# Two-layer decoder kernel: the order of work on all five engines and the buffer slots come from a list scheduler in the kernel

## The chip, the cores and the metric

The kernel runs on one core of one Trainium2 chip. The metric is the device time of one execution in microseconds (us); the number compared is the median over several executions. Engines are named as in the profile: PE is the matrix engine (TensorE), with PEld for its weight loads; DVE is VectorE, ACT is ScalarE, POOL is GpSimd, and SP is the engine that issues nearly all DMA transfers.

## The reference

The kernel computes a two-layer decoder trunk for one sequence of 256 positions and width 1024, in float32. Each layer mixes tokens, then runs a SwiGLU block, each with a residual scaled by alpha and a LayerNorm:

```python
for i in range(DEPTH):                       # DEPTH = 2
    if i % N_MIXERS == 0:                    # layer 0: gated MLP over positions
        h = x @ a_w_in[li]
        u, v, q_mem = jnp.split(h, [W_MIX, 2 * W_MIX], axis=-1)
        mix = gmlp_mixer(u, v, a_ln_v_g[li], a_ln_v_b[li], a_w_s[li], a_b_s[li])
    else:                                    # layer 1: causal attention, 12 heads of 64
        h = x @ b_w_in[li]
        q, k, v, q_mem = jnp.split(h, [W_MIX, 2 * W_MIX, 3 * W_MIX], axis=-1)
        mix = moba_attention(q, k, v)        # 256 positions: one block, so plain causal
    mem_out = memory_cross_attention(q_mem, mem, w_mem_kv[i])   # 4 heads, 256 memory tokens
    sub = jnp.concatenate([mix, mem_out], axis=-1) @ w_mix_out[i]
    x = layer_norm(ALPHA * x + sub, ln_mix_g[i], ln_mix_b[i])
    x = layer_norm(ALPHA * x + swiglu(x, w_ffn_in[i], w_ffn_out[i]), ln_ffn_g[i], ln_ffn_b[i])
```

`gmlp_mixer` is gelu(u) * (W_s layer_norm(gelu(v)) + b_s), with a causal 128 x 128 matrix W_s for each of 12 groups; `swiglu` is (silu(g) * u) @ w_out with an inner width of 2816.

## The kernel before, in words

**Split weights.** PE works on float32 data in three passes. Every operand is split into a high part, which ACT makes by a cast to a shorter float type (line 248, `scalar.copy`), and a low part, which DVE makes by subtracting the high part from the original (line 249, `vector.tensor_sub`). A product is then high x high, high x low and low x high, all added up in PSUM. So every weight tile passes DMA, then ACT, then DVE, before PE can use both parts. Nearly all of the 117 MB that are read are weights; most come in tiles of 128 x 2048 floats (1 MB), each split in two halves of 128 x 1024.

**Tiles by name.** A tile `raw_x` is what a DMA loaded, and `spl_x_0`, `spl_x_1` are its two split halves. In the order of use: `raw_v0` to `raw_v3` (projection v of layer 0), `qm0` (memory queries), `u0` to `u2` (projection u), `km0` and `vm0` (memory keys and values; the memory tokens come as `mraw0` to `mraw3`), `o0_0` to `o0_3` (output projection), then the feed-forward weights of layer 0. Layer 1 has `bv0` to `bv3`, `qk0` to `qk5` (queries and keys, one tile for each pair of heads) and `o1_0` to `o1_3`. `wsT` and `vn<-in_bs` are the spatial matrices and broadcast biases of the gated MLP, and `gv` its norm's gain and shift.

**Keys with their low part.** Attention scores use stacked tiles: ACT casts the keys out of PSUM twice (lines 478 and 479, tiles `kkm` and `qks`), and DVE subtracts to get the low part, `klm` for the memory keys and `klq` for attention (line 480). The score product (tile `sm` or `s`) reads them at once.

**Feed-forward chunks.** The inner width is worked off in 11 chunks of 256. Chunks marked R are plain products; those marked S (four in each layer) use seven products M1 to M7 of sums of weight blocks (`raw_s1_7_11`, `_12`, `_21`, `_22` for layer 1, chunk 7). The sums are made in place by DVE (line 199, 128 x 2048) and by one accumulating DMA from POOL (line 202). Results of the products are joined by DVE at lines 625 to 636: tiles `m1g`, `u2g`, `m5g` for the gate half, and `m1f`, `m5f` for the other.

**What sets the order.** PE's order is that of the program text (`manual_schedule` for PE alone). The other engines' order is chosen by the framework's own scheduler, from the dependencies and from rotating pools: 4 raw tiles, 10 split tiles, 9 work tiles, and 4 + 4 PSUM tiles. At the output projection of layer 1, `stream.behind` with `issue_after` holds some splits behind named exponentials (line 206). Each engine works through its queue strictly in order, so an instruction that waits holds all that stand behind it on that engine. All loads named here are issued on SP's queue, save the accumulating ones.

## Time and profile before

| what | value |
| --- | --- |
| median of 3 runs | 563.2 us (562.88, 563.20, 563.69) |
| span of the profiled execution, first to last instruction | 561.0 us |
| around the span, against the median | 2.2 us (the profile gives no time of its own for that execution) |
| PE busy | 550.9 us, 98% of the span |
| PE weight loads busy | 478.4 us, 85% |
| DVE busy | 500.5 us, 89% |
| ACT busy | 360.1 us, 64% |
| POOL busy | 22.4 us, 4% |
| DMA | 118.88 MB, mean 212 GB/s |
| granted PE clock | 0.998 of full speed, mean over the core's span |

A row of the waits view reads: the engine that waited, the tile it was to produce and its line, the engine and tile waited for, then the time in total, how many times, and the longest. A row of the timeline reads: start and duration in us, engine, line, operation, output<-inputs, shapes and count (several instructions of one kind in a row are one row), and in brackets the idle time before it with what ended it. A row of the windows view gives for a stretch of time the busy time and instructions of each engine, the granted clock, the mean busy share of the 16 DMA engines, and what they moved in GB/s.

### The profile page before, as it was taken

What the parts mean: (1) busy time and instruction counts of PE and PEld (TensorE: products, weight loads), DVE (VectorE), ACT (ScalarE), POOL (GpSimd) and SP (SyncE); (2) the same over time, 40 slices, a digit from 0 to 9 for tenths busy, and PEclk for the clock granted to TensorE, in tenths of its full rate; (3) what the DMA queues carried; (4) which work ended last, traced back from release to release, by engine and by line L of the source; (5) the groups of instructions that cost most, each with busy time, mean ns of one, the idle gap of its engine ahead of it and who ended that gap; (6) DMA issues with size and microseconds to landing.
All of it is one profiled execution on the core that took longest, in us unless ns stands there. A gap on an engine that the chain in (4) does not pass through costs nothing.

```text
span 561.0 us, 8037 instructions
## 1 busy us (share of the span) xinstructions
PE 550.9 (98%) x3052; PEld 478.4 (85%) x3052; DVE 500.5 (89%) x667; ACT 360.1 (64%) x550; POOL 22.4 (4%) x32
## 2 busy tenths in 40 slices
PE   8999999999999999999999999999999999999994
PEld 8999979888888888888899999788888887888883
DVE  5897999999998999995987879789998997999985
ACT  6766947767655766863466879765676674765910
POOL 2020000000000000000000000000000000000001
PEclk9999999999999999999999999999999999999999
DMA  8997794548756486598477222367258766485602
GB/s 291 399 324 308 250 369 170 208 77 313 210 206 247 112 325 161 192 335 296 140 240 297 75 77 76 142 254 280 85 152 316 197 249 217 133 307 145 225 1 75
DMA packets 21623, 118.88 MB, mean 212 GB/s; under 512 B 2384, under 2 KB 6096, under 8 KB 9168
## 3 DMA queue, kind: packets, MB, share of 16 engines
q1 hardware_dynamic: 20000, 109.45, 52.8%
q0 software_dynamic: 1152, 8.39, 8.1%
q8 instruction: 24, 0.39, 0.3%
q10 hardware_dynamic: 432, 0.52, 0.3%
q14 instruction: 15, 0.12, 0.1%
HBM read 117.31 MB, written 1.05 MB: 211 GB/s over the span
## 4 chain that ended last, share of the span: by engine, by line
PE 85%; DVE 7%; ACT 3%; DMA 2%; issue 2%; SPq 1%; DVEq 0%; ACTq 0%
PE fof L272 11%; PE fog L272 8%; PE Xf L272 8%; PE pg L272 6%; PE pf L272 6%; PE Xg L272 5%; PE opc L272 4%; PE opa L272 4%; PE Zf L272 4%; PE qk L272 4%; PE pu L272 3%; PE bv L272 3%; PE Zg L272 3%; PE pvm L272 3%; PE va L272 2%; PE hkm L272 2%
## 5 line engine op out<-in xcount | busy, mean ns | idle before, releaser
L248 ACT CAST spl_s_M<-raw_s 128x1024 fp32r<-128x1024 f32 x112 | 114.4, 1052 | 56.7 <-DVE raw_s L199 41.9
L249 DVE TENSOR_TENSOR spl_s_M<-raw_s,spl_s_M 128x1024 fp32r<-128x1024 f32 x112 | 132.6, 1217 | 7.7 <-ACT spl_s_M L248 7.5
L272 PE MATMUL fof<-spl_w,htf 128*128 128x512 f32 x264 | 63.8, 392 | 0.0
L272 PE MATMUL fog<-spl_w,htg 128*128 128x512 f32 (+1 forms) x282 | 63.7, 378 | 0.0
L272 PEld LDWEIGHTS fog<-spl_w,htg 128*128 128x128 f32 x282 | 50.2, 188 | 9.4
L272 PEld LDWEIGHTS fof<-spl_w,htf 128*128 128x128 f32 x264 | 49.0, 188 | 10.0
L199 DVE TENSOR_TENSOR raw_s<-raw_s,raw_s 128x2048 f32<-128x2048 f32 x24 | 54.8, 2284 | 0.2
L249 DVE TENSOR_TENSOR spl_w<-raw_w,spl_w 128x1024 fp32r<-128x1024 f32 x44 | 53.0, 1217 | 1.2 <-ACT spl_w L248 1.1
L248 ACT CAST spl_w<-raw_w 128x1024 fp32r<-128x1024 f32 x44 | 45.4, 1050 | 4.7 <-PE fog L272 1.9
L272 PE MATMUL qk<-x2T,spl_qk 128*128 128x256 f32 x288 | 36.3, 283 | 0.0
L272 PEld LDWEIGHTS qk<-x2T,spl_qk 128*128 128x128 f32 x288 | 35.2, 192 | 0.0
L272 PE MATMUL Xf<-spl_s_M,SfM 128*128 128x512 f32 x96 | 23.1, 389 | 0.0
L272 PE MATMUL opc<-spl_o,mix 128*128 128x512 f32 x96 | 23.1, 394 | 0.0
L272 PE MATMUL Zf<-spl_s_M,SfM 128*128 128x512 f32 x96 | 23.1, 389 | 0.0
L272 PE MATMUL Zg<-spl_s_M,SgM 128*128 128x512 f32 x96 | 23.1, 389 | 0.0
L272 PE MATMUL Xg<-spl_s_M,SgM 128*128 128x512 f32 x96 | 23.1, 389 | 0.0
L272 PE MATMUL Xg<-spl_s_M,x3T 128*128 128x512 f32 x96 | 22.7, 391 | 0.2 <-DVE m5g L632 0.2
L272 PE MATMUL Xf<-spl_s_M,x1T 128*128 128x512 f32 x96 | 22.6, 389 | 0.0
L272 PE MATMUL opa<-spl_o,mix 128*128 128x512 f32 x96 | 22.5, 392 | 0.0
L272 PEld LDWEIGHTS Xg<-spl_s_M,x3T 128*128 128x128 f32 x96 | 17.9, 188 | 4.4 <-DVE m5g L632 0.6
L272 PEld LDWEIGHTS Xf<-spl_s_M,SfM 128*128 128x128 f32 x96 | 18.0, 188 | 3.8
L272 PEld LDWEIGHTS Xg<-spl_s_M,SgM 128*128 128x128 f32 x96 | 18.0, 188 | 3.7
(245 smaller groups left out, 1080.2 us busy)
## 6 DMA issues: line engine op xcount, KB each, us to landing
raw_s<-in_w SPq DMA_DIRECT2D x32, 1024.0 KB, 5.1
raw_w<-in_w SPq DMA_DIRECT2D x22, 1024.0 KB, 4.8
raw_o<-in_w SPq DMA_DIRECT2D x8, 1024.0 KB, 6.3
raw_s<-in_w POOLq DMA_DIRECT2D x8, 1024.0 KB, 7.9
raw_r_A<-in_w SPq DMA_DIRECT2D x6, 1024.0 KB, 4.9
raw_r_B<-in_w SPq DMA_DIRECT2D x6, 1024.0 KB, 6.0
raw_qk<-in_w SPq DMA_DIRECT2D x6, 1024.0 KB, 5.5
raw_u<-in_w SPq DMA_DIRECT2D x3, 1024.0 KB, 9.2
```

Source lines behind the costliest of these rows:

```text
L199: self.nc.vector.tensor_add(self.raw[parts[0]], self.raw[parts[0]], self.raw[parts[1]])
L248: nc.scalar.copy(hi, src)
L249: nc.vector.tensor_sub(lo, src, hi.bitcast(F32))
L272: nc.tensor.matmul(o, lhsT, rhs, start=start, stop=stop, skip_group_check=on)
```

## The change

All of `build` is now recorded before it is issued. `nc` becomes a `Plan`: each call makes an `Op` with its engine, its operands, the operations that must precede it (found by overlap of the bytes of its operands) and a cost from a formula. `tile_of` makes a `Buffer` with a tag and a number of slots. At the end `nc.emit()` finds an order and issues it.

- `deadlines` goes along PE's order, which stays the program's, and gives each PE operation a time; then it goes backwards and gives every other operation the latest time by which it must start.
- `simulate` runs the machine by the cost formulas. At each step an engine takes, among operations that can start, the one with the earliest deadline; it may put in a shorter one, or wait a little, for a more urgent one that is about to be ready. Five sets of three limits are tried, and the order in which PE loses least is kept.
- A transfer is modelled as 2300 ns and a shared link at 437 bytes per ns.
- `emit` issues the operations in that order on all five engines (`manual_schedule` names all five), with a pool slot of its own for each tag and slot number, chosen by the same model.
- `stream.behind` and its `issue_after` are gone, since the order is explicit.

The methods `either`, `copy` and `scale`, which would let the scheduler choose between two engines, are not called; every operation stays on its engine, and PE's sequence is that of before.

```diff
 class Plan:
+    TRIALS = ((150, 1500, 800), (150, 1000, 500), (300, 1500, 1200), (100, 700, 300), (300, 2500, 1600))
...
+    def delay(self, a, b):
+        if a.engine == b.engine and a.name != "dma_start":
+            return a.hold
+        if a.name == "dma_start":
+            return 2300 + a.bytes / 400 if a.engine != "gpsimd" else 2300 + a.bytes / 180
+        return a.lat + (50 if b.engine == "tensor" else 33)
+
+    def deadlines(self):
+        t = 4300
+        for op in self.ops:
+            if op.engine == "tensor":
+                op.late = t
+                t += op.hold
...
+        for op in reversed(self.ops):
+            late = [o.late - self.delay(op, o) for o in op.after if o.late is not None]
+            late += [follow[b].late - self.delay(op, follow[b]) for b in op.roots if b in follow]
...
+            op.late = min(late) if late else t
...
+    def simulate(self, slip, idle, margin):
...
+                t0 = min(t for t, _ in c)
+                first = [x for x in c if x[0] <= t0 + 1]
+                t, op = min(first, key=lambda x: (x[1].late, x[1].n))
...
+            if op.name == "dma_start":
+                size = op.bytes * (2.1 if e == "gpsimd" else 1) / 437
+                link = max(link, t + 2300) + size
+                end = max(link, t + 7800 if e == "gpsimd" else 0) + 100
+            else:
+                end = t + op.call.lat
...
+    def emit(self):
...
+        for op in self.order():
+            for b in op.opens:
+                b.tile = self.pools[b.pool].tile(b.dims, b.dtype, tag=f"{b.tag}_{b.slot}", name=b.name, bufs=1)
+            c = op.call
+            getattr(getattr(self.nc, c.engine), c.name)(*map(real, c.args), **{k: real(v) for k, v in c.kw.items()})
...
-        if key in self.behind:
-            with self.tc.issue_after(self.behind[key]):
-                self.split(hl[:, 0, :n], hl[:, 1, :n], raw)
-        else:
-            self.split(hl[:, 0, :n], hl[:, 1, :n], raw)
+        self.split(hl[:, 0, :n], hl[:, 1, :n], raw)
...
-        tc.manual_schedule(engines={ET.PE}),
+        tc.manual_schedule(engines={ET.PE, ET.DVE, ET.Activation, ET.Pool, ET.SP}),
...
-        stream.behind = {(f"o1_{k}", x): prs[p][1].exp.ins for k, p in ((0, 2), (1, 3), (3, 4)) for x in range(2)}
```

Three places of the new order follow. In the rows the first item is the source line; after the change all recorded operations are issued by one helper, so they all have line 527. The number at the end of a tile's name is that of the buffer.

**SP, the first loads after those of projection v.** Before:

```order
L185 DMA raw_qm0_294<-in_w 128x2048
L185 DMA raw_u0_296<-in_w 128x2048
L185 DMA raw_u1_298<-in_w 128x2048
L185 DMA raw_u2_300<-in_w 128x2048
L185 DMA raw_km0_308<-in_w 128x2048
L768 DMA gv_310<-in_a_ln_v_g 128x768
L773 DMA mraw0_313<-in_memT 128x2x256
L781 DMA wsT_322<-in_wsT 128x1536
L789 DMA wsT_322<-in_bs 64x256 x4
L789 DMA vn_321<-in_bs 64x256 x2
L185 DMA raw_vm0_419<-in_w 128x2048
```

SP in the same place after the change:

```order
L527 DMA raw_qm0_192<-in_w 128x2048
L527 DMA mraw0_197<-in_memT 128x2x256
L527 DMA wsT_221<-in_wsT 128x1536
L527 DMA raw_u0_228<-in_w 128x2048
L527 DMA wsT_221<-in_bs 64x256 x4
L527 DMA vn_253<-in_bs 64x256
L527 DMA raw_u1_260<-in_w 128x2048
L527 DMA raw_u2_279<-in_w 128x2048
L527 DMA gv_285<-in_a_ln_v_g 128x768
L527 DMA raw_km0_321<-in_w 128x2048
L527 DMA raw_vm0_394<-in_w 128x2048
```

Rows that only repeat are left out: the second `gv`, `mraw1` to `mraw3`, and in the new order the second `vn<-in_bs`, between `raw_u1` and `raw_u2`. The same transfers stand between `raw_qm0` and `raw_vm0`, but `mraw`, `wsT` and the broadcasts have moved ahead of `raw_u0` to `raw_u2`, and `raw_km0` is the last of them instead of the fourth.

**DVE ahead of the memory scores.** Before, from the splits of `vm0` to the fourth `klm`:

```order
L249 TENSOR_TENSOR spl_vm0_0_730<-raw_vm0_419,spl_vm0_0_730 128x1024
L249 TENSOR_TENSOR spl_vm0_1_745<-raw_vm0_419,spl_vm0_1_745 128x1024
L249 TENSOR_TENSOR spl_o0_0_0_849<-raw_o0_0_478,spl_o0_0_0_849 128x1024
L249 TENSOR_TENSOR spl_o0_0_1_858<-raw_o0_0_478,spl_o0_0_1_858 128x1024
L480 TENSOR_TENSOR klm_126<-hkm0_591,kkm00_589 64x256
L828 TENSOR_TENSOR gt0_689<-sv0_680,wsT_322 128x512
L828 TENSOR_TENSOR gt1_705<-sv1_696,wsT_322 128x512
L480 TENSOR_TENSOR klm_126<-hkm0_591,kkm00_589 64x256
```

DVE after the change, from the splits of `km0` on; `vn` is the norm of the gated MLP:

```order
L527 TENSOR_TENSOR spl_km0_0_473<-raw_km0_321,spl_km0_0_473 128x1024
L527 TENSOR_TENSOR spl_km0_1_485<-raw_km0_321,spl_km0_1_485 128x1024
L527 BN_AGGR mvv0_514<-stv0_354 128x2
L527 SCALAR_TENSOR_TENSOR vn_253<-vn_253,mvv0_514,gv_285 128x768
L527 TENSOR_TENSOR spl_vm0_0_504<-raw_vm0_394,spl_vm0_0_504 128x1024
L527 TENSOR_TENSOR spl_o0_0_0_542<-raw_o0_0_437,spl_o0_0_0_542 128x1024
L527 TENSOR_TENSOR spl_o0_1_0_570<-raw_o0_1_468,spl_o0_1_0_570 128x1024
L527 TENSOR_TENSOR spl_o0_2_0_620<-raw_o0_2_521,spl_o0_2_0_620 128x1024
L527 TENSOR_TENSOR spl_o0_3_0_685<-raw_o0_3_600,spl_o0_3_0_685 128x1024
L527 TENSOR_TENSOR klm_116<-hkm0_635,kkm00_701 64x256
L527 TENSOR_TENSOR gt0_719<-sv0_698,wsT_221 128x512
L527 TENSOR_TENSOR klm_116<-hkm0_635,kkm01_722 64x256 x2
```

Left out are the second halves of `vm0`, `o0_0`, `o0_1` and `o0_2`, the second pair of statistics, three more `vn` steps, and the second `klm`, right behind `gt0`. Seven halves of `o0` now stand ahead of the first `klm` (two before), together with the `km0` splits and four `vn` steps, which before were over earlier; the second `gt` products and the `mix` splits that stood between the `klm` are behind them now.

**DVE at feed-forward chunk 7 of layer 1.** Before:

```order
L629 TENSOR_TENSOR u2g5_4444<-u2g5_4444,Zg5_4298 128x512
L630 SCALAR_TENSOR_TENSOR m1g5_4317<-m1g5_4317,u2g5_4444 128x512
L249 TENSOR_TENSOR spl_s1_7_M1_0_4534<-raw_s1_7_11_4510,spl_s1_7_M1_0_4534 128x1024
L249 TENSOR_TENSOR spl_s1_7_M1_1_4543<-raw_s1_7_11_4510,spl_s1_7_M1_1_4543 128x1024
L249 TENSOR_TENSOR spl_w1_4_1_4568<-raw_w1_4_4336,spl_w1_4_1_4568 128x1024
L199 TENSOR_TENSOR raw_s1_7_11_4510<-raw_s1_7_11_4510,raw_s1_7_12_4512 128x2048
L632 TENSOR_TENSOR m5g5_4370<-m5g5_4370,Xg5_4296 128x512
```

After the change:

```order
L527 TENSOR_TENSOR spl_s1_7_M1_0_4458<-raw_s1_7_11_4423,spl_s1_7_M1_0_4458 128x1024
L527 TENSOR_TENSOR spl_s1_7_M1_1_4464<-raw_s1_7_11_4423,spl_s1_7_M1_1_4464 128x1024
L527 TENSOR_TENSOR m1g5_4343<-m1g5_4343,Yg5_4416 128x512
L527 TENSOR_TENSOR u2g5_4481<-u2g5_4481,Zg5_4375 128x512
L527 TENSOR_TENSOR raw_s1_7_11_4423<-raw_s1_7_11_4423,raw_s1_7_12_4381 128x2048
L527 SCALAR_TENSOR_TENSOR m1g5_4343<-m1g5_4343,u2g5_4481 128x512
L527 TENSOR_TENSOR spl_w1_4_1_4473<-raw_w1_4_4280,spl_w1_4_1_4473 128x1024
L527 TENSOR_TENSOR m5g5_4398<-m5g5_4398,Xg5_4321 128x512
```

The two M1 splits have moved ahead of `u2g`; the sum of line 199 and the split of `w1_4` still stand ahead of `m5g`. SP now issues `raw_s1_7_11`, which M1 needs, ahead of `raw_s1_7_22` instead of behind it, and the sum that frees its slot stands earlier on DVE.

Two smaller moves are the `klq` steps (line 480) of attention. For the first pair of heads both stood around `spl_qk5_1` (one before it, one behind), and now both stand ahead of it. For pair 4 DVE had `klq`, the copy `pTm12`, `spl_o1_1_1`, `klq`, and now has `spl_o1_2_0`, `klq`, `klq`, `pTm12`; ACT likewise makes all four key and query casts of that pair right after one split.

More of the change, by code (lines that the diff above doesn't have):

```diff
@@ new lines, with __init__ @@
+class Buffer(View):
+    def __init__(self, pool, space, tag, bufs, shape, dtype, name):
+        n = 1
+        for s in shape[1:]:
+            n *= s
+        ap = space[:P * n].rearrange("(p n) -> p n", p=P)
+        if len(shape) > 2:
+            names = "abcd"[:len(shape) - 1]
+            ap = ap.rearrange(f"p ({' '.join(names)}) -> p {' '.join(names)}", **dict(zip(names, shape[1:])))
+        super().__init__(None, ap)
+        self.pool, self.tag, self.bufs, self.dims, self.dtype, self.name = pool, tag, bufs, list(shape), dtype, name
+        self.psum, self.whole = pool == "ps", False
+        self.tile, self.log, self.slot, self.left, self.last = None, [], None, 0, 0.0
@@ new lines, with __init__, calls, cost @@
+class Op:
+    def __init__(self, n, engine, name, args, kw):
+        self.n, self.engine, self.name, self.args, self.kw = n, engine, name, args, kw
+        out = kw["out"] if "out" in kw else args[0]
+        views = [v for v in [*args, *kw.values()] if isinstance(v, View)]
+        self.writes = [v for v in (out, kw.get("accum_out")) if isinstance(v, View)]
+        self.reads = [v for v in views if not any(v is w for w in self.writes)]
+        self.before, self.after, self.opens = {}, [], []
+        self.late, self.other = None, None
+        self.cost()
+    def calls(self):
+        return {o.engine: o for o in (self, self.other) if o}
+    def cost(self):
+        w = max([v.width() for v in self.writes + self.reads] or [1])
+        e, n = self.engine, self.name
+        if n == "dma_start":
+            v = (self.writes or self.reads)[0]
+            self.bytes = 4 * v.ap.ap[0][1] * v.width()
+            self.hold, self.lat = (900 if e == "gpsimd" else 400), 0
+        elif e == "tensor":
+            w = self.args[2].width() if n == "matmul" else P
+            f32 = n == "matmul" and self.args[2].root.dtype == F32
+            self.hold = max(104, (w + 32) / 2.4) if not f32 else 0.85 * w
+            self.lat = 200 + 0.37 * w if not f32 else self.hold + 270
+        elif e == "vector":
+            slow = n in ("tensor_scalar_mul", "tensor_scalar_add") or n == "tensor_copy"
+            self.lat = 225 + 0.48 * w if n == "tensor_scalar_mul" and w > 8 else 150 + 1.042 * w
+            self.hold = self.lat - 82
+        elif e == "scalar":
+            self.lat = 190 + 0.842 * w + (200 if "accum_out" in self.kw else 0)
+            self.hold = self.lat - 100
+        else:
+            self.lat = self.hold = 700 + 2.5 * w if w < 8 else 250 + 2.0 * w
@@ L178, in load_ahead @@
                 self.held.add(tag)
[L179 removed]
+                raw = self.tile("act", [P, 2, D], F32, tag, f"raw_{name}").rearrange("p a c -> p (a c)")
             else:
@@ L293, in build @@
             pattern=[[0, 2], [-1, P]], channel_multiplier=1)
-        klm, klq = (const.tile([P, 2, 2, T], F32R, name=n) for n in ("klm", "klq"))
+        klm, klq = (const_tile([P, 2, 2, T], F32R, n) for n in ("klm", "klq"))
         for kl in (klm, klq):
@@ L493, in mem_q @@
         def mem_q(name, xs):
-            qa = [actp.tile([P, 2, T], F32R, tag=f"qm{c}", name=f"q{name}{c}") for c in range(2)]
+            qa = [tile_of("act", [P, 2, T], F32R, f"qm{c}", f"q{name}{c}") for c in range(2)]
             t = proj_t(name, xs)
@@ L500, in mem_k @@
         def mem_k(name, memx):
-            ka = [actp.tile([P, 2, T], F32R, tag=f"mix{6 + c}", name=f"k{name}{c}") for c in range(2)]
+            ka = [tile_of("act", [P, 2, T], F32R, f"mix{6 + c}", f"k{name}{c}") for c in range(2)]
             t = proj_t(name, memx)
@@ L887, in build @@
         qm = mem_q("qm1", xs)
-        mix = [actp.tile([P, 2, T], F32R, tag=f"mix{k}", name=f"mix1_{k}") for k in range(6)]
+        mix = [tile_of("act", [P, 2, T], F32R, f"mix{k}", f"mix1_{k}") for k in range(6)]
         qks, prs, pTs = {}, {}, {}
@@ L969, in build @@
             p.normalise()
-        stream.behind.update({("o1_2", x): prs[5][1].exp.ins for x in range(2)})
         op.step(0, [2, 3])
@@ L978, in build @@
         op.step(1, [0, 1, 2, 3])
-        x3T = actp.tile([P, KT, 2, T], F32R, tag="xT", name="x3T")
+        x3T = tile_of("act", [P, KT, 2, T], F32R, "xT", "x3T")
         A = {}
```

358 lines of the change are left out of this document (314 added, 44 removed).

## The prediction, on record before the result

> **What bounds the kernel now.** I read the page's sums first, then what PE waits for, then the timeline around each wait.
>
> ```profile
> span 561.0 us, 8037 instructions
> PE 550.9 (98%) x3052; PEld 478.4 (85%) x3052; DVE 500.5 (89%) x667; ACT 360.1 (64%) x550; POOL 22.4 (4%) x32
> PE 85%; DVE 7%; ACT 3%; DMA 2%; issue 2%; SPq 1%; DVEq 0%; ACTq 0%
> ```
>
> PE is busy for 98% of the span and is 85% of the chain that ended last. The change leaves every engine its instructions and PE its sequence, so it can win only what PE loses by waiting, and can lose whatever it makes PE wait for. The waits of PE, with the total, the number of times and the longest:
>
> ```profile
> PE warmup L284 <- DVE mhalf L281: 1.1, 1, 1.1
> PE va L272 <- ACT spl_v L248: 0.6, 1, 0.6
> PE s L272 <- DVE klq L480: 0.6, 2, 0.4
> PE Xg L272 <- DVE m5g L632: 0.2, 1, 0.2
> ```
>
> The first two lie in the start of the program. The last two lines are three waits for DVE far inside it. A wait costs more than its bracket, as the starts of the matmuls show:
>
> ```profile
> 308.59 0.23 PE L272 MATMUL s<-qks 128*128 128x128 f32 x1
> 309.04 0.33 PE L272 MATMUL s<-klq,qks 128*128 128x128 f32 x1 [0.22 <-DVE klq L480]
> 344.58 0.29 PE L272 MATMUL s<-qks 128*128 128x128 f32 x1
> 345.23 0.33 PE L272 MATMUL s<-klq,qks 128*128 128x128 f32 x1 [0.36 <-DVE klq L480]
> 470.89 2.88 PE L272 MATMUL fog<-spl_w,htg 128*128 128x512 f32 x12
> 473.98 3.25 PE L272 MATMUL Xg<-spl_s_M,x3T 128*128 128x512 f32 x13 [0.21 <-DVE m5g L632]
> ```
>
> From 308.59 to 309.04 is 0.45, where matmuls of this size follow each other by about 0.11: 0.34 lost. Likewise 0.65 − 0.11 = 0.54. Thirteen Xg matmuls take 3.25 with the last one's pipeline tail; at about 0.226 each the twelve before them end their issue at 470.89 + 2.71 = 473.60, so 0.38 is lost. **Sum: 0.34 + 0.54 + 0.38 = 1.26 us**, the whole of what a better order can win behind the start.
>
> **The change part by part: the three waits.** What DVE did just before each:
>
> ```profile
> 306.50 0.42 DVE L480 TENSOR_TENSOR klq<-qk,qks 64x256 fp32r<-64x256 f32 x1
> 307.30 1.23 DVE L249 TENSOR_TENSOR spl_qk<-raw_qk,spl_qk 128x1024 fp32r<-128x1024 f32 x1 [0.38 <-ACT spl_qk L248]
> 308.56 0.43 DVE L480 TENSOR_TENSOR klq<-qk,qks 64x256 fp32r<-64x256 f32 x1
> 343.51 1.21 DVE L249 TENSOR_TENSOR spl_o<-raw_o,spl_o 128x1024 fp32r<-128x1024 f32 x1
> 344.75 0.43 DVE L480 TENSOR_TENSOR klq<-qk,qks 64x256 fp32r<-64x256 f32 x1
> 466.27 0.69 DVE L629 TENSOR_TENSOR u2g<-u2g,Zg 128x512 f32<-128x512 f32 x1 [2.50 <-ACT u2g L617]
> 467.63 2.36 DVE L249 TENSOR_TENSOR spl_s_M<-raw_s,spl_s_M 128x1024 fp32r<-128x1024 f32 x2
> 471.05 2.28 DVE L199 TENSOR_TENSOR raw_s<-raw_s,raw_s 128x2048 f32<-128x2048 f32 x1
> 473.25 0.68 DVE L632 TENSOR_TENSOR m5g<-m5g,Xg 128x512 f32<-128x512 f32 x1
> 466.55 2.00 ACT L248 CAST spl_s_M<-raw_s 128x1024 fp32r<-128x1024 f32 x2 [0.31 <-DMA raw_s<-in_w]
> ```
>
> *First klq.* The second one stood behind a 1.23 split that itself waited 0.38 for ACT. In the new order both stand ahead of it, so the second ends about 1.23 + 0.38 earlier, near 307.4, and PE wants it at 308.7: the 0.34 goes. The split becomes later by one klq, 0.4; its weights are wanted only after the scores.
>
> *Second klq.* The new order takes the split (1.21) and the copy ahead of it out from between the two, and gives ACT's four casts one run. The gain of at least 1.21 is over 0.54: gone. The split of o1 that is now behind is for a product that starts later.
>
> *m5g.* Between u2g and m5g stood two M1 splits (2.36), one more split and the sum (2.28). The M1 splits could not go earlier, because their raw tile landed at 466.5 (the ACT row, "DMA raw_s"). Now its slot is freed sooner and it is issued ahead of a 1 MB neighbour, one transfer earlier (1.05 MB is 2.7 to 4.0 us at the 384 and 262 GB/s quoted below); M1 then fits in DVE's 2.50 of idle time before u2g. If all of it fits, m5g ends 2.36 − 0.1 earlier, near 471.7. If the tile lands only 2 us earlier, at 464.5, the two casts and subtractions end near 467.6 and m5g comes out near 473.6, just when PE wants it. Either way most of 0.38 goes; I take all of it, with 0.3 as the uncertainty.
>
> Elsewhere the feed-forward chunks are reordered too, with the same instructions. No gain is left there, since the list of waits names no other. A loss would be one long instruction put ahead of a result that PE waits for: 1.2 for a split, 2.3 for a sum, less the slack that the result had. I take 0, because in the old order one result in all S chunks of both layers was late, by 0.38; the cover is the slack of the others, and a chunk that overran it would pay the excess.
>
> **The part that costs: the head, 18 to 59 us.** Here the SP order moves raw_km0 from fourth to last in its set, and DVE, which takes instructions strictly in order, has the km0 splits ahead of everything else up to the memory scores.
>
> ```profile
> 18.20 2.00 ACT L248 CAST spl_qm<-raw_qm 128x1024 fp32r<-128x1024 f32 x2 [1.64 <-DMA raw_qm<-in_w]
> 32.78 1.22 SPq L789 DMA_DIRECT2D vn<-in_bs x2
> DMA to landing us min/median/max: 6.7/6.9/7.2
> 18.20:29.20 11.00, 11.00 (x82) 11.00 (x82) 9.02 (x10) 9.34 (x13) 0.00 (x0) 1.00 0.99 384
> 29.20:40.20 11.00, 11.00 (x94) 11.00 (x93) 10.75 (x18) 7.54 (x13) 3.51 (x3) 1.00 1.06 315
> 34.00:40.00 6.00, 6.00 (x53) 6.00 (x52) 5.94 (x8) 3.12 (x7) 1.32 (x1) 1.00 1.07 262
> ```
>
> raw_qm0 lands at 18.2 in both. The last of the set in the old order are the two vn<-in_bs (the landing row is theirs): the second is issued at 33.5 and lands 6.7 later, at 40.2. So the set takes 22.0 us. In the new order raw_km0 is the end of the same set. Call its landing L. Upper end: the same packets take the same time, L = 40.2. Lower end: the set is 7.2 MB (four 1.05, mraw 1.05, wsT 0.79, gv 0.79, broadcasts 0.39), which at the 384 GB/s of the first window takes 18.8, L = 37.0. I take 39.5, near the upper end: in the second window the DMA engines were not idle (share 1.06) and yet moved only 315, so slow packets, not gaps, cost the time, and those packets are still there.
>
> What must follow on DVE before the scores:
>
> ```profile
> L248 ACT CAST spl_s_M<-raw_s 128x1024 fp32r<-128x1024 f32 x112 | 114.4, 1052 | 56.7 <-DVE raw_s L199 41.9
> 47.51 2.36 DVE L249 TENSOR_TENSOR spl_vm<-raw_vm,spl_vm 128x1024 fp32r<-128x1024 f32 x2 [3.38 <-ACT spl_vm L248]
> 42.00 1.00 DVE L816 SCALAR_TENSOR_TENSOR vn<-vn,mvv,gv 128x768 f32<-128x768 f32 x1
> 52.48 0.42 DVE L480 TENSOR_TENSOR klm<-hkm,kkm 64x256 fp32r<-64x256 f32 x1 [0.33 <-ACT kkm L479]
> 52.82 1.48 DVE L828 TENSOR_TENSOR gt<-sv,wsT 128x512 f32<-128x512 f32 x2
> 58.15 0.43 DVE L480 TENSOR_TENSOR klm<-hkm,kkm 64x256 fp32r<-64x256 f32 x1 [0.26 <-ACT kkm L479]
> 28.46 17.44 PE L272 MATMUL pu<-x0T,spl_u 128*128 128x256 f32 x144
> 57.95 0.28 PE L272 MATMUL sm<-klm,qqm 128*128 128x256 f32 x1
> 58.91 0.28 PE L272 MATMUL sm<-klm,qqm 128*128 128x256 f32 x1
> ```
>
> After L: one cast, 1.07 with its start; eleven subtractions (two each for km0, vm0, o0_0, o0_1, o0_2, one for o0_3) at 1.14 from start to start, 12.6 in all; four vn steps at 0.95, 3.8; two pairs of small statistics, 0.45 together. That is L + 17.9. Then klm, gt, klm, klm, klm: the first is done at L + 18.4, the second at L + 19.3 (0.6 for gt, 0.35 for klm), the fourth at L + 20.0. The second is the tightest. PE started its matmul at 57.95, so it wants it at 57.9. Lateness: 39.5 + 19.3 − 57.9 = **0.9 us**; by the ends of L it is 0 (any L below 38.6) to 1.6. The fourth is late by 39.5 + 20.0 − 58.9 = 0.6, which is not added: once PE has been held, its later needs move with it. In the old order the fourth klm ended at 58.58 and was in time by 0.3.
>
> raw_u0 is the other load at risk. Ahead of it now come mraw and wsT, 1.84 MB; with its own 1.05 it lands at 18.2 + 2.88 MB at 384 GB/s = 25.7, or 27.3 at 315. PE starts pu at 28.46 and needs the low half by 28.7; cast, subtraction and their starts take 2.3, so a landing by 26.4 costs nothing: 0 to 0.9, say 0.1. A PE that is held here is later at the scores as well, so the head costs the larger of the two, not the sum: 0.9.
>
> A rule of the Trainium skill bears on L: "DMA: Bandwidth & Descriptors", section on queues, rings and completion order, says that each DMA engine takes the descriptors of one ring in order, though they may complete out of order. By it a load queued behind raw_km0 can't delay it, and 40.2 is a firm upper end. The same page's section on bandwidth puts the memory side of one core near 358 GB/s; an estimate by that figure gives 18.2 + 7.2/0.358 = 38.3 for L, no lateness, and a time 1.26 lower than before. The first window's 384 is above that figure, so I don't go by it.
>
> The very start (0 to 13 us) swaps halves of raw_v0 with x0raw; the loads' sum is equal, I bound it by ±0.3 and take 0. The end of the program, behind the last matmul, keeps its order.
>
> **Sum.** −1.26 + 0.9 = −0.36, on the span 561.0 − 0.36 = 560.6. The median of the runs stands 2.2 above the profiled span (563.2), which covers what lies around it: 563.2 − 0.4 = **562.8 us**. A change of less than 0.2% (1.1 us) can't be told from none by these measurements, so this is no change.
>
> **The rivals.**
>
> *The head costs nothing.* If the broadcasts' slow packets are spread among the large loads and overlap with them, L is 38.6 or less and the klm are in time; only −1.26 is left: 561.9. For it: 384 GB/s in the first window; of the 3.2 us between the set's 22.0 and its 18.8, 1.6 would have to go. Against it: the DMA share of 1.07 at 262 GB/s in the slow stretch. The limit of "faster" is a head cost of 0.13, L = 38.7.
>
> *The broadcasts slow their neighbours.* wsT, the broadcasts and their slow stretch now stand among raw_u0 and raw_u1. If everything from wsT to raw_u1 (3.2 MB) moves at the 262 GB/s of the slow stretch, it takes 12.2 instead of 8.4, 3.8 more, of which the old order already paid 1.9 (6 us at 262 instead of 384). Then L = 40.2 + 1.9 = 42.1, klm is late by 3.5, and the sum is −1.26 + 3.5 = +2.2: 565.4. It decides from L = 41.0 on, where the head costs 2.4 and the whole is slower by 0.2%. For it: klm has eleven splits and four vn steps ahead of it in one queue and no way round. Against it: in the old order the neighbours before and after that stretch moved at 384 and more.
>
> *The order isn't kept in effect.* If the three waits only move (klq late for ACT, m5g for its raw tile) and the head costs 0.9, the time is 564.1; that is still no change, at the edge.
>
> **How the numbers follow.** No change (L between 38.7 and 41.0, and the third rival): 0.38, with its own range 562.1 to 564.3. Head free: 0.36. Neighbours slowed, or another order that holds PE by over 2.4: 0.26. The predicted time is that of the likeliest, 562.8. The range takes 0.6 below the free head for the start's ±0.3 and waits of the start, 561.3, and reaches just past the slowed neighbours, 565.6. Faster 0.36, same 0.38, slower 0.26.
>
> **What would show it.** PE's waits should no longer name klq (first and fifth pair) or m5g. raw_km0 should land at 39 to 40 and the first klm should start near 57.5, directly behind the split of o0_3, with PE waiting for klm near 58 for about 0.9. If klm starts before 57 the head was free; if PE waits for spl_u or for klm by over 2 us, the slowed neighbours were right. The prediction is wrong at its root if PE waits appear in the feed-forward chunks, where I priced the reordering at nothing.

## The result, and the profile after

The changed kernel takes 569.74 us (median of 4 runs, 568.96 to 570.6), the kernel before takes 563.45 us in the same job (562.88 to 563.72). The ratio is 1.0117, with an interval of 1.0103 to 1.0132: slower by 1.2%. Forecast was 562.8 us, no change, with a range that ended at 565.6. The time lies above the range, by 4.1 us.

The profiled execution of the changed kernel took 569.77 us, its span is 568.1 us. The sums of the page, with the chain that ended last:

```profile
span 568.1 us, 8078 instructions
PE 554.7 (98%) x3052; PEld 478.0 (84%) x3052; DVE 498.8 (88%) x667; ACT 363.6 (64%) x550; POOL 23.0 (4%) x32
PE 47%; DVE 25%; issue 5%; DMA 4%; ACT 3%; DVEq 0%; ACTq 0%
```

DVE and ACT have as much work as before. PE's share of the chain has gone from 85% to 47%, and DVE's from 7% to 25%: PE now waits for results that it used to find ready. The waits of PE behind the start (total, times, longest):

```profile
PE sm L527 <- DVE klm L527: 0.6, 1, 0.6
PE Xf L527 <- ACT u2f L527: 0.6, 1, 0.6
PE pu L527 <- DVE spl_u L527: 0.5, 1, 0.5
PE tpf L527 <- DVE hf L527: 0.4, 1, 0.4
PE tpf L527 <- DVE m5f L527: 0.4, 1, 0.4
PE pf L527 <- DVE x1T L527: 0.3, 1, 0.3
PE Xg L527 <- ACT u2g L527: 0.3, 1, 0.3
PE tpg L527 <- DVE hg L527: 0.2, 1, 0.2
PE pt L527 <- DVE mix L527: 0.2, 1, 0.2
```

Of the four rows of before, klq and m5g are gone. In their place stand nine small ones, at nine places of the program. None is over 0.6 us.

PE runs the same 3052 matmuls in the same order in both kernels, so the start of each can be set against its start before. The difference is PE's lag, and its steps show where time is lost or won. The steps of over 0.2 us, each from the matmul before it to where the lag is level again (times on the clock of the changed kernel):

| place | step of the lag, us |
| --- | --- |
| start, 7 to 12 us (va, for its split weights) | +0.7 |
| 30.0, pu for spl_u | +0.77 |
| 59 to 62, sm for klm | +2.1 |
| 106, pf for x1T | +0.56 |
| 119 and 131, tpf for hf | +0.31 and +0.66 |
| 190, tpf for m5f | +0.62 |
| 211 and 217, Xf for u2f and m5f | +0.83 and +0.29 |
| 290, turn of the layers (ptb) | −0.32 |
| 315, s for klq, first pair | −0.44 |
| 339 and 342, qk and pt for mix | +0.40 and +0.39 |
| 351.5, s for klq, pair 4 | −0.64 |
| 405, tpg for hg | +0.47 |
| 480, Xg for m5g | −0.49 |
| 506 and 512, Xg for u2g and m5g | +0.53 and +0.29 |

The head costs 3.5 us in all, the rest of layer 0 another 3.4 (3.3 in these steps), layer 1 costs 2.1. The three forecast gains are there (−1.57 together), and one of −0.32 that I had not seen. The end is at +7.2.

**The head.** Rows of the timeline of the changed kernel (start, duration, engine, line, operation, and in brackets the idle time before it with what ended it), in the order in which they matter:

```profile
39.51 2.00 ACT L527 CAST spl_km<-raw_km 128x1024 fp32r<-128x1024 f32 x2 [1.84 <-DMA raw_km<-in_w]
...
47.69 0.43 SPq L527 DMA_DIRECT2D gb0mix<-in_ln_mix_b  x1
49.58 0.33 SPq L527 DMA_DIRECT2D raw_o<-in_w  x1
...
56.19 1.05 ACT L527 CAST spl_o<-raw_o 128x1024 fp32r<-128x1024 f32 x1 [4.29 <-DMA raw_o<-in_w]
58.98 1.13 ACT L527 CAST kkm<-hkm 64x256 fp32r<-64x256 f32 x3 [0.70 <-DVE klm L527]
...
57.27 1.23 DVE L527 TENSOR_TENSOR spl_o<-raw_o,spl_o 128x1024 fp32r<-128x1024 f32 x1 [0.91 <-ACT spl_o L527]
58.53 0.42 DVE L527 TENSOR_TENSOR klm<-hkm,kkm 64x256 fp32r<-64x256 f32 x1
58.87 0.67 DVE L527 TENSOR_TENSOR gt<-sv,wsT 128x512 f32<-128x512 f32 x1
60.15 0.43 DVE L527 TENSOR_TENSOR klm<-hkm,kkm 64x256 fp32r<-64x256 f32 x1 [0.60 <-ACT kkm L527]
61.01 0.42 DVE L527 TENSOR_TENSOR klm<-hkm,kkm 64x256 fp32r<-64x256 f32 x1 [0.43 <-ACT kkm L527]
61.86 0.43 DVE L527 TENSOR_TENSOR klm<-hkm,kkm 64x256 fp32r<-64x256 f32 x1 [0.43 <-ACT kkm L527]
```

raw_km0 is there at 39.4, as forecast. Two other things make klm late. First, raw_o0_3 is issued at 49.58, now with the two gb0mix broadcasts ahead of it on SP. ACT is idle for 4.29 us until it lands. Its casts and subtractions stood behind the keys' before; now the first of each stands ahead of the casts of the keys and of klm. Second, ACT and DVE take turns: ACT's fourth key cast waits 0.70 for the first klm, DVE's second klm waits 0.60 for ACT's casts, and the third and fourth wait 0.43 each. A klm comes every 0.85 us, where its own work is 0.43. All these casts and klm read one PSUM tile, hkm. That a klm waits for a cast can be for its own input; that a cast waits for a klm can't, since the klm writes nothing that the cast reads and reads nothing that it overwrites. So in the built program an ACT step and a DVE step on one PSUM tile wait for each other in the order in which they were emitted, though both only read it. The scheduler's plan has no such rule: for two readers it records no dependency.

The Trainium skill states a reason for such a rule, in "PSUM — Partial Sum Buffer", section "PSUM bank collisions raise a hardware error": two engines must not touch one bank at a time in the same group of 32 partitions, two readers included, and the compiler's scheduler makes them wait for each other. The cast that waits 0.70 for a klm agrees with it.

**The feed-forward of layer 0.** One of its waits, for u2f, which ACT copies out of PSUM; the rows are SP's, ACT's and PE's of the changed kernel:

```profile
198.82 0.33 SPq L527 DMA_DIRECT2D raw_w<-in_w  x1
201.03 6.60 SPq L527 DMA_DIRECT2D raw_s<-in_w  x3
...
207.52 2.00 ACT L527 CAST spl_s_M<-raw_s 128x1024 fp32r<-128x1024 f32 x2 [4.09 <-DMA raw_s<-in_w]
209.43 1.04 ACT L527 CAST spl_w<-raw_w 128x1024 fp32r<-128x1024 f32 x1
210.37 0.57 ACT L527 COPY u2f<-Xf 128x512 f32<-128x512 f32 x1
...
211.00 3.02 PE L527 MATMUL Xf<-spl_s_M,SfM 128*128 128x512 f32 x12 [0.56 <-ACT u2f L527]
```

The transfer issued at 201.03 (raw_s0_8_11) lands 6.4 us later. ACT is idle for 4.09 us and then makes three casts, and the copy that PE needs stands behind them. The wait of tpf for m5f has the same shape on DVE: a pair of splits stands ahead of the join.

```profile
187.36 2.36 DVE L527 TENSOR_TENSOR spl_s_M<-raw_s,spl_s_M 128x1024 fp32r<-128x1024 f32 x2
189.63 0.69 DVE L527 SCALAR_TENSOR_TENSOR m5f<-m5f,sgf 128x512 f32<-128x512 f32 x1
```

In the order of issue on SP, raw_w0_6 has moved ahead of that tile:

```
before                     after
raw_s0_8_12                raw_s0_8_12
raw_s0_8_11                raw_w0_6
raw_w0_6                   raw_s0_8_11
raw_s0_8_22                raw_s0_8_22
```

The scheduler issues first what can start first, which on SP means the tile whose buffer is free. The deadline decides only between tiles that are free at the same time.

### The profile page after: what moved, and what is told of

Same layout as the page of the kernel before. It is cut to its first block, busy times and chain, and to the rows that moved or that the text cites. A ratio compares the mean times of both kernels' runs of the same rounds, so it can differ in the third digit from the quotient of the medians.

```text
span 568.1 us, 8078 instructions
## 1 busy us (share of the span) xinstructions
PE 554.7 (98%) x3052; PEld 478.0 (84%) x3052; DVE 498.8 (88%) x667; ACT 363.6 (64%) x550; POOL 23.0 (4%) x32
## 4 chain that ended last, share of the span: by engine, by line
PE 47%; DVE 25%; issue 5%; DMA 4%; ACT 3%; DVEq 0%; ACTq 0%
PE fog L527 7%; PE fof L527 7%; DVE spl_s_M L527 6%; PE Xg L527 5%; PE Xf L527 4%; DMA raw_s<-in_w 4%; DVE raw_s L527 4%; PE opc L527 4%; PE bv L527 3%; PE qk L527 3%; PE pg L527 2%; PE Zf L527 2%; PE pf L527 2%; PE Zg L527 2%; DVE spl_w L527 1%
```

## The experiments

Two theories of the loss stand against each other, and a third came with the second set. The first blames the **plan's blindness to PSUM turns**: it doesn't know that ACT and DVE wait for each other on a PSUM tile, so klm, x1T, hf and mix come later than planned. The second blames the **price of a load**: the plan gives it 2.3 us plus its bytes, and broadcasts no more than others, so that what depends on loads (o0_3, u2f, m5f) comes later than planned. The third blames the **order of issue on SP**, by readiness and not by deadline. All kernels below compute the full reference.

The lag of PE at five matmuls, named by their start in the kernel before, serves all of them (in us, from one profiled execution each; the last column is the measured median against the median before of the same job):

| kernel | 50 us | 64 us | 230 us | 360 us | end | ratio of the medians, interval |
| --- | --- | --- | --- | --- | --- | --- |
| the change | 1.4 | 3.5 | 6.9 | 6.3 | 7.2 | 1.0117 (1.0103 to 1.0132) |
| PSUM turns in the plan | 0.8 | 4.3 | 5.1 | 3.6 | 4.1 | 1.0088 (1.0063 to 1.0113) |
| dearer loads in the plan | 5.7 | 5.6 | 6.5 | 5.9 | 5.4 | 1.0105 (1.009 to 1.012) |
| both | 6.9 | 6.9 | 6.9 | 5.5 | 5.0 | 1.0068 (1.0049 to 1.0088) |
| one o0_3 split behind klm | 1.7 | 1.8 | 4.7 | 4.1 | 4.5 | 1.011 (1.0093 to 1.0127) |
| SP by deadline | 1.3 | 1.3 | 2.9 | 2.2 | 2.2 | 1.0028 (1.0017 to 1.0039) |
| SP by deadline, PSUM turns | 0.8 | 0.8 | 1.6 | 0.1 | −0.4 | 0.9987 (0.9978 to 0.9996) |
| SP by deadline, PSUM turns, dearer loads | 0.3 | 0.9 | 0.9 | −0.6 | −1.2 | 0.9972 (0.9958 to 0.9986) |
| the same, first loads in program order | 0.2 | 0.2 | 0.1 | −1.3 | −1.8 | 0.9961 (0.9946 to 0.9976) |
| SP by deadline, first loads in program order | 0.0 | 0.3 | 2.2 | 1.6 | 1.6 | 1.0019 (1.001 to 1.0029) |
| that, with PSUM turns | 0.3 | 0.3 | 1.0 | −0.5 | −1.0 | 0.9971 (0.9958 to 0.9985) |
| that, with dearer loads | 0.0 | 0.5 | 1.6 | 0.9 | 0.4 | 0.9996 (0.9985 to 1.0007) |

### The plan knows the turns on a PSUM tile

```diff
         def opening(op):
             t0 = at[op.n]
+            for b in op.roots:
+                if b.psum and op.engine in by_late:
+                    t0 = max(t0, touched.get((b, "scalar" if op.engine == "vector" else "vector"), 0.0))
...
             op.end = end
+            for b in op.roots:
+                if b.psum and op.engine in by_late:
+                    touched[b, op.engine] = end + 33
```

> The scheduler is told one more rule: a step of ACT or DVE that touches a PSUM tile can't start before the other engine's last planned step on that tile has ended. Nothing else is changed; the plan is made anew. Theory W (the plan is wrong because it doesn't know that these two engines wait for each other on a PSUM tile): the klm are no longer late by alternation (about 1.7 us of the 2.1 us that klm costs in the changed kernel) and DVE has no 1.3 us lag at 100 us, so x1T and hf of chunk 0 and 1 (0.66, 0.32 and 0.59) come in time: 569.7 - 3.3 = 566.4 us. Theory D (the plan is wrong because transfers land later than it thinks): the waits at u0, klm, m5f and u2f remain and the time stays within 1 us of 569.7.

Measured: 567.32 us (566.34 to 569.74; before 562.6). That is 4.7 over the kernel before instead of 6.3. The waits for x1T, mix and hg are gone, and one of the two for hf. Those for u2f and m5f don't appear either: from 64 to 230 us the lag grows by 0.8 instead of 3.4. But they are not won by the rule. SP issues all its loads in the order of the change, and from 150 to 218 us the order of ACT, DVE and POOL is that of the change too. The two tiles that these waits go back to (issued at 168.4 and 201.0 in the change, the second is raw_s0_8_11) took 5.5 us each from issue to landing in this execution, and 6.4 in that of the change. So of the 3.4 lost in the rest of layer 0, 1.7 (m5f and u2f) hang on how fast single loads land, in an order that leaves them no room. The wait for klm stays, now in one piece, since four klm stand in a row behind the splits of raw_o0_3. The timeline of PE:

```profile
58.14 0.28 PE L534 MATMUL sm<-kkm,qqm 128*128 128x256 f32 x1
60.18 0.39 PE L534 MATMUL sm<-klm,qqm 128*128 128x256 f32 x1 [1.76 <-DVE klm L534]
...
61.78 0.41 PE L534 MATMUL sm<-klm,qqm 128*128 128x256 f32 x1
61.99 0.41 PE L534 MATMUL sm<-kkm,qqm 128*128 128x256 f32 x1
```

After that wait the matmuls follow each other by 0.21, where they did by 0.12: PE runs at a lower clock for some us, which adds 1.6. The scores now cost 3.5 instead of 2.1, where 1.7 less was expected, and the median gains 1.6 and not 3.3. The first theory explains the x1T and one hf in layer 0 (0.9), the mix and hg in layer 1 (1.3), and by itself nothing of the head.

### The plan's loads cost more

```diff
-            return 2300 + a.bytes / 400 if a.engine != "gpsimd" else 2300 + a.bytes / 180
+            return 3800 + a.bytes / 400 if a.engine != "gpsimd" else 3800 + a.bytes / 180
...
-                link = max(link, t + 2300) + size
+                link = max(link, t + 3800) + size
...
+            src = self.args[1].ap.ap if isinstance(self.args[1], View) else self.args[1].ap
+            if any(p[0] == 0 and p[1] > 1 for p in src):
+                self.bytes *= 2
```

> The scheduler's price of a transfer is raised: 3800 ns instead of 2300 ns ahead of the bytes, and twice the bytes for a source row that is broadcast. The plan is made anew. Theory D: loads are issued earlier or their splits placed later, the waits for u2f (0.77), u2g (0.41), m5f (0.63 and 0.32) and part of klm (1.0, the late o0_3) go: 569.7 - 3 = 566.7 us. Theory W: x1T, hf and the alternation of klm stay, and the time stays above 568.5 us.

Measured: 568.6 us (568.0 to 569.31), 6.0 over the kernel before. The waits for u2f, u2g, m5f and m5g are gone, with them the second hf and hg, which the second theory doesn't name; the steps for x1T (0.57), one hf (0.31) and mix (0.40 and 0.37) stay. For u2f the order has changed here: one cast stands ahead of the copy instead of three. A source that is broadcast counts with twice its bytes in this plan. But the new prices moved SP's order in the head: raw_qm0 now stands behind mraw and wsT, and the lag is 5.7 before the scores are reached. The two waits of PE there:

```profile
PE hqm L530 <- ACT spl_qm L530: 2.9, 1, 2.9
...
PE hqm L530 <- DVE spl_qm L530: 0.8, 1, 0.8
```

Behind the head the lag falls by 0.2 to the end, so the second theory may have its part too; the gain is eaten by a new wait at another place. The time lies where the first theory put it, but for a reason that neither theory had.

### Both

The edits of the two kernels above together.

> Both edits of the scheduler's model together: the PSUM rule and the slower transfers. If the two theories are each half of the truth, the gains add: 569.7 - 6 = about 563.5 us, the time of the kernel before, and PE's waits behind the start sum to under 1 us. If neither is the cause (the order is bad for another reason, such as no margin at all), it stays above 567 us.

Measured: 566.52 us (565.24 to 567.98). From 50 us to 230 us the lag doesn't grow at all, and then it falls by 1.9. With both edits nothing is lost behind the head any more, and the whole loss is in the head, before 50 us. The time is 3.9 over the kernel before: neither the 563.5 of two half theories nor above 567. The waits there:

```profile
PE hqm L537 <- ACT spl_qm L537: 2.1, 1, 2.1
...
PE hqm L537 <- DVE spl_qm L537: 0.8, 1, 0.8
```

SP issues raw_qm0 behind five loads that were ready earlier and are needed later, since it goes by readiness. This led to the third theory.

### The order of the change, with one split moved

Here the order is not planned anew. It is the order of the change, with the cast and the subtraction of the first half of o0_3 moved behind the key casts and behind klm.

```diff
+        seq = self.order()
+        behind("scalar", "spl_o0_3_0", 0, "kkm01", -1)
+        behind("vector", "spl_o0_3_0", 0, "klm", 3)
-        for op in self.order():
+        for op in seq:
```

> The changed kernel's order is kept on all engines but for one thing: the cast (ACT) and the subtraction (DVE) of the first half of o0_3 stand behind the memory keys' steps kkm and klm instead of ahead of them. If the late load of o0_3, with the alternation of kkm and klm behind it, is what makes klm late, PE's wait for klm goes altogether, 2.1 us: 567.6 us. If klm is late because DVE has too much to do before it, only 0.5 us are won: 569.2 us.

Measured: 568.59 us (567.13 to 569.57), 6.0 over the kernel before instead of 6.3. The wait for klm is gone, which shows that the split of raw_o0_3 caused it: the lag is the same at 64 us as at 50 us. The turns are still there (the later klm wait 0.61, 0.43 and 0.44 for ACT) and cost PE next to nothing without the late load. But the median gains only 0.3 of the 2.1, which the intervals of the two ratios can't tell from none. A part goes to a new wait, for pTm. It stands behind two km1 splits on DVE as it did in the change; PE, 1.7 us less late at this place, now comes before it (timeline of DVE, then the waits of PE):

```profile
56.61 0.42 DVE L536 TENSOR_TENSOR klm<-hkm,kkm 64x256 fp32r<-64x256 f32 x1
...
73.61 2.36 DVE L536 TENSOR_TENSOR spl_km<-raw_km,spl_km 128x1024 fp32r<-128x1024 f32 x2
75.88 1.29 DVE L536 COPY pTm<-ptm 128x512 f32<-128x512 f32 x2
```

```profile
PE pvm L536 <- DVE pTm L536: 1.0, 1, 1.0
```

The profiled execution shows neither u2f nor m5f waiting, though the order is that of the change: the tile raw_s0_8_11 took 5.3 us from issue to landing here and 6.4 there. With the first experiment that makes two executions of this order without those waits: whether they appear depends on single loads. The profiled execution is the fastest of the four (567.13), so its lag of 4.5 at the end is not that of the median.

### SP strictly by deadline

```diff
+        line = sorted((o for o in self.ops if o.engine == "sync"), key=lambda o: (o.late, o.n))
...
                 else:
                     cands = ready[e]
+                if e == "sync" and line:
+                    cands = [line[0]] if line[0] in cands else []
...
             gone.add(op)
+            if e == "sync":
+                line.remove(op)
```

> The scheduler is told one rule: SP issues its transfers strictly in the order of their deadlines, and holds the queue while the next one's buffer isn't free, instead of issuing whatever could start first. (Before, SP put mraw, wsT and the broadcasts ahead of raw_u0 because their buffers were free some us earlier.) The model's prices and rules are those of the changed kernel. If the order of the head's loads is the cause of the waits at u0 (0.64) and klm (2.1), both go and the rest stays: the kernel before + 6.3 - 2.7 = + 3.6 us. Rival: holding the queue makes loads late in the feed-forward chunks, or the klm stay late by their alternation with ACT: + 5 us or more.

Measured: 564.68 us (564.01 to 565.0; before 562.84), 1.8 over the kernel before. One rule of the plan takes away 4.5 of the 6.3. The waits of PE:

```profile
PE va L532 <- ACT spl_v L532: 1.2, 1, 1.2
PE tpf L532 <- DVE hf L532: 0.4, 1, 0.4
PE tpg L532 <- DVE hg L532: 0.3, 1, 0.3
PE pf L532 <- DVE x1T L532: 0.3, 1, 0.3
PE pt L532 <- DVE mix L532: 0.2, 1, 0.2
```

klm is gone, and with it spl_u and all of u2f, u2g, m5f and m5g. What is left behind the start is what the first theory names and the second hf. More went than I had expected (+3.6): I had left u2f and its kin to the price of a load. In the order of issue raw_s0_8_11 stands ahead of raw_w0_6 again. So the price and the order of issue can be two ways to the same end: either more time is planned for a late tile, or it is issued earlier. How much of the 4.5 is u2f and m5f, which two executions of the old order didn't have, is not known; u0 and klm alone were 2.9 in the profile of the change.

### By deadline, with the PSUM turns, and with dearer loads

The edits above together: first the deadline with the PSUM turns, then with the dearer loads as well.

> SP by deadline and the PSUM rule of the first experiment together, the price of a transfer as in the changed kernel. The waits left in the first experiment behind the head were hf (0.63), u2g (0.42) and m5g (0.31); with the head's 4 us gone and the three won waits (1.3) kept: the kernel before + 0.5 us, between 0 and + 1.5. If the late transfers matter more without the head's delay (PE is then earlier against the loads): + 2 us.

> As the one above, but the first loads also by deadline, which puts a half of raw_v0 ahead of x0raw, as the changed kernel does. It prices the start alone: in the changed kernel PE was 0.7 us later than before after the first 12 us. Expected: 0.7 us slower than the kernel with the first loads in program order; within 0.2 if the start is only noise.

Measured: 562.11 us (561.38 to 562.95) and 561.25 us (560.32 to 563.29). The first is under the kernel before by 0.7 us or 0.1%, with an interval just below 1, where + 0.5 (0 to + 1.5) was expected: u2g and m5g are gone too, and the gains at klq, m5g and ptb are 1.9 and not 1.3. Of its waits behind the start only one for hf is left. The steps for x1T, the first hf, mix and hg, 2.1 in all, which the kernel by deadline alone still has, are gone with the rule, and the median falls by 2.6. In the second PE waits 0.3 for klm, and loses nothing between 64 and 230 us.

### The start

These two kernels lose 0.8 and 0.3 at the start, where the deadlines put halves of raw_v0 ahead of x0raw. The next kernel issues the first loads in program order:

```diff
-key=lambda o: (o.late, o.n)
+key=lambda o: (0 if o.writes and o.writes[0].root.name[:5] in ("x0raw", "raw_v")
+               and o.writes[0].root.name not in ("raw_vm0", "raw_vm1") else o.late, o.n)
```

> All three rules (SP by deadline, PSUM rule, slower transfers), and the first sixteen loads (x0raw and raw_v) in program order. No wait in the feed-forward chunks was left with the two model rules, so with the head's loads in order only the gain of the three removed waits should remain: the kernel before - 1.3 us, 0.2% faster. Rival: a list scheduler without slack in its plan loses 1 us somewhere else on the chip whatever it is told: the kernel before + 0 to + 1.

> SP by deadline with the first sixteen loads in program order, and no other edit of the changed kernel's scheduler. If the two edits of SP's order add, it is 0.8 us faster than SP by deadline alone (that profile shows PE 1.4 us later after the start, the one with program order 0.3): the kernel before + 0.8 us. The waits for x1T, hf, hg and mix (about 2.8 us in all) have to be there still, since the plan doesn't know the PSUM rule.

Measured: 560.8 us (560.12 to 561.72) for all edits with this start, 2.0 under the kernel before where 1.3 was expected (again by the 1.9 of the gains), and 0.45 less than with the start by deadline, where 0.7 was expected; the intervals of the two overlap. And 564.13 us (563.07 to 565.37; before 562.99) for the deadline and this start alone, 1.1 over the kernel before where it was 1.8 without it. The waits for x1T, hf, hg and mix are all still there, as expected, and small ones for klm (0.4) and pTm (0.3) came in. The start is worth 0.45 to 0.7; the change lost 0.7 there in its profile. One execution says little on this: over the eight profiles with a start by deadline the lag at 12 us goes from 0.1 to 1.6, with a mean of 0.75, and over the five with program order from 0.0 to 0.2.

### One edit at a time on this base

> As above with the PSUM rule. Only the wait for hf at chunk 1 (0.6) should be left: the kernel before - 1.0 us. If the gain of the PSUM rule was an accident of another plan, it stays at + 0.5.

> SP by deadline, first loads in program order and the slower transfers, without the PSUM rule. If the slower price does a share of its own, the hf wait goes and x1T, mix and hg stay: the kernel before - 0.2 us. If the two model edits cover the same waits, it equals the one with all rules, - 2 us.

Measured: 561.75 us (561.23 to 562.67) with the PSUM turns, 562.88 us (561.86 to 564.48) with dearer loads, both close to what was expected (− 1.0 and − 0.2; measured − 1.2 and − 0.1). The first has the one wait that was forecast. In the second the number came right with other waits than forecast: x1T and hg went, one hf (0.75) and mix stayed, and klm and pTm came in. That price alone is thus the price of another order, and no proof of the second theory. Against 564.13 without either, the PSUM turns are worth 2.4 and the price 1.25; with the other in place, by the kernel measured next, 2.1 and 1.0.

### All edits, measured again

The kernel of all edits with program order at the start, five rounds.

> The kernel with all rules once more, in five rounds, for its interval against the kernel before: 0.4% faster as in the first measurement (0.25 to 0.55%).

Measured: 560.77 us (560.73 to 561.23), ratio 0.9955 (0.9942 to 0.9968): faster than the kernel before by 0.45%, and than the change by 1.6%. Its span is 559.0 us. The waits of PE, the only row:

```profile
PE warmup L692 <- DVE mhalf L689: 1.1, 1, 1.1
```

And the place where ACT and DVE took turns in the memory of layer 1 (timelines of DVE and ACT, first of the change, then of this kernel):

```profile
100.71 0.41 DVE L527 TENSOR_TENSOR klm<-hkm,kkm 64x256 fp32r<-64x256 f32 x1
101.55 0.43 DVE L527 TENSOR_TENSOR klm<-hkm,kkm 64x256 fp32r<-64x256 f32 x1 [0.43 <-ACT kkm L527]
102.41 0.86 DVE L527 TENSOR_TENSOR klm<-hkm,kkm 64x256 fp32r<-64x256 f32 x2 [0.44 <-ACT kkm L527]
```

```profile
94.70 3.02 ACT L542 CAST kkm<-hkm 64x256 fp32r<-64x256 f32 x8 [0.39 <-PE hkm L542]
...
98.37 1.72 DVE L542 TENSOR_TENSOR klm<-hkm,kkm 64x256 fp32r<-64x256 f32 x4
```

Eight casts in one run and then four klm in one run, with no idle time between them. In the change the turns made DVE lose 0.87 here, and x1T and hf, behind them on DVE, came late. The steps for x1T and the first hf (together 0.8 to 0.9) stand in the change, by deadline alone, and by deadline with program order; with the PSUM turns added, both are gone each time.

**The account.** Against the kernel before, by medians: the change +6.3; SP by deadline −4.5; program order at the start −0.45 to −0.7; the PSUM turns −2.1 to −2.6; dearer loads −0.9 to −1.25. With the +6.3 they add up to −1.7 to −2.75; measured is −2.0 and −2.2. Along one path the steps add up by construction; what is not by construction is that the price of the PSUM turns came out much the same on three bases and that of the loads on three.

**What stays open.** Each edit to the plan's rules makes a new order throughout, so each price is that of a whole new order; that a mechanism is behind it rests on which waits vanish. For the PSUM turns these waits fit the price; for the dearer loads they do so only with the other edits in place, where the wait for the second hf (0.65) goes. Only the kernel with the one moved split kept the order. How often the waits for u2f and m5f appear in the change, and how much of its median they make up, can't be read from one profiled execution of each kernel.

## Why the prediction was wrong

**The three waits: right, and a little low.** Forecast −0.34, −0.54 and −0.38, together −1.26; measured −0.44, −0.64 and −0.49, together −1.57. The working by what stands ahead of klq and m5g on DVE held. Each is 0.1 more than I had, in part because the matmul behind the one that waited had started late too.

**The turn of the layers: missed.** −0.32 at ptb. My rows of the waits of before have none for it, so "the whole of what a better order can win behind the start" was too little by that.

**L: right.** raw_km0 lands at 39.43, where I took 39.5. The slowed neighbours, the rival that would have explained a slower kernel, needed 42.1: its sign came true, its mechanism didn't.

**What must follow on DVE before the scores: the first step that failed.** I had the klm done at L + 18.4 to L + 20.0, and took the second as the tightest, late by 0.9. Measured, the first is done at 58.95, L + 19.5, and the fourth at 62.29, L + 22.9, and the fourth is the tightest: its matmul starts at 62.34 where it was 58.91 before, 3.4 late. Two things make the klm later than I had them. I followed raw_km0 and not the load behind it, raw_o0_3, for which ACT stood idle until 56.19 (about 1.1). And I gave the last klm their own 0.35, where each waits for a cast of ACT: 0.60 + 0.43 + 0.43. I had read such a row in the profile of before, "[0.33 <-ACT kkm L479]", and taken it for a cast that was not yet done, not for a rule. The kernel with the one moved split shows which of the two PE pays for: without the late load the turns cost it next to nothing. The sentence that the head costs the larger and not the sum did hold: the 0.7 of the start and the 0.77 of raw_u0 lie inside the 3.4.

**raw_u0: right in the landing, low in the price.** It came at 27.6 (forecast 25.7 to 27.3), and PE lost 0.77; the bounds were 0 to 0.9, and I took 0.1.

**The start: wrong.** ±0.3, taken as 0, measured +0.7 (0.75 in the mean of eight executions with such a start). The sum of the loads was equal, but PE waits there for the first split of raw_v and for x0T, which comes from x0raw, each 0.4.

**"Elsewhere the feed-forward chunks are reordered too … I take 0": the step that failed by most.** Measured: 3.4 in the rest of layer 0 and 2.1 in layer 1, 5.5 us in all, of which 1.7 came with loads that landed late in this one execution. My reason was that in the old order only one result of all S chunks was late. That is a fact about the old order's slack. The new order has its own, and its plan leaves little: it counts a result as in time if it is ready when PE wants it by the plan's prices. Every price that is too low, and every wait that the plan doesn't know, then shows on PE. The rows of DVE ahead of m5f show the pattern that I had named as a loss and priced at nothing: two splits of 1.2 ahead of a 0.69 join that PE waits for. The prediction said that it would be wrong at its root if waits appeared there, and it is.

With these terms in place of mine, the sum closes: head 3.5, rest of layer 0 and layer 1 5.5, gains −1.57 and −0.32: +7.1, the difference of the spans (568.1 − 561.0 = 7.1). Without the 1.7 of the late loads the time would still lie above the range, at 568.0.

## What to carry to other kernels

An order from a scheduler with a model is as good as the model: before its prices are believed, look in the profile of the old order for what the model doesn't have (turns on a PSUM tile in the brackets of ACT and DVE, the landing times of loads), and give an order with no slack a loss for each place where it may be late, not zero. Loads should be issued by when they are needed, not by when a buffer is free; here that one rule made 4.5 of 6.3 us. Where a wait is removed by moving one instruction, look for the next one in the row: moving one split took away 2.1 us of waiting, and the median gained 0.3, not clear of noise. And before a vanished wait is put down to an edit, see whether the edit changed the order at that place: u2f and m5f vanished in two kernels whose order there was the same.

## What the hardware showed unexpectedly

A wait of PE of about 2 us can cost much more than itself, because the granted clock can fall behind it. The windows view (start and end, length, busy time of PE, PEld, DVE, ACT, POOL with instructions, granted clock, DMA share, GB/s) of the kernel with the PSUM turns, around its wait of 1.76 at 58.4 to 60.2, and of the kernel with both edits, around its wait of 2.07 that ends at 25.8:

```profile
56.00:60.00 4.00, 2.42 (x21) 2.22 (x19) 3.40 (x5) 3.88 (x12) 0.00 (x0) 1.00 0.99 389
60.00:64.00 4.00, 3.82 (x19) 3.82 (x20) 3.88 (x9) 1.72 (x4) 0.00 (x0) 0.57 1.00 353
64.00:68.00 4.00, 4.00 (x29) 3.74 (x29) 4.00 (x10) 3.84 (x12) 0.00 (x0) 1.00 0.93 343
```

```profile
26.00:30.00 4.00, 3.25 (x15) 3.04 (x16) 2.93 (x4) 3.77 (x5) 0.00 (x0) 0.53 1.03 311
30.00:34.00 4.00, 4.00 (x24) 4.00 (x23) 3.95 (x5) 3.80 (x6) 0.00 (x0) 0.62 1.00 407
```

The clock is 0.57 for one window and then 1.00 again in the first kernel, and 0.53 and 0.62 for two windows in the second; the lag grows by 1.6 and by 2.7 us in that time, behind waits that cost 1.9 and 3.3 themselves (2.07, and 0.76 just behind it). In the change, whose waits there are each 0.6 or less, the windows at the same place show 1.00 throughout. It doesn't always happen: the kernel with the one moved split waits 1.67 us at the start, up to 10.29, and its clock stays at 1.00:

```profile
8.00:12.00 4.00, 2.31 (x12) 1.65 (x10) 1.73 (x4) 2.69 (x5) 0.00 (x0) 1.00 1.04 384
```

So the small waits cost what they are here, and a long one can cost more.

The Trainium skill has a rule on this, in "TensorE: Matmul & The Clock Gate", section "Part 1: The HAM clock gate": PE falls to half its clock after an idle window of about 3.4 us. The half agrees with the rows. The length doesn't: here 1.76 and 2.07 us of waiting were followed by the drop and 1.67 were not, and no run shows where the limit lies.
